# The gates' bias, added by matmuls or by accumulating transfers, in a one-core hybrid mixer layer

## The chip, the core and the metric

The kernel runs on one core of a Trainium2 chip. The metric is the device time of one execution in microseconds (us); lower is better. Five engines work from queues of their own, each in its queue's order: TensorE (PE in the profile, its weight loads PEld), VectorE (DVE), ScalarE (ACT), GpSimd (POOL) and SyncE (SP). They wait for each other, and for transfers, through semaphores.

## The reference, cut to what matters

One decoder layer on 256 tokens of width 2048: four token mixers run on a normalised, modulated input `h`, each is projected to 2048 channels and multiplied by a gate of its own, and the sum goes through an output projection and a SwiGLU feed-forward part. The gates are what the change is about:

```
h = _rms(x, norm_g[l, 0]) * (1.0 + scale_m) + shift_m
merged = [jax.nn.sigmoid(h @ w_gate[l, i] + b_gate[l, i]) * (branches[i].astype(h.dtype) @ w_branch[l, i])
          for i in range(N_BRANCH)]
mix = (merged[0] + merged[1] + merged[2] + merged[3]) @ w_out[l]
```

`w_gate` is four matrices of 2048 x 2048, and `b_gate` four rows of 2048, one number for each channel and the same for every token.

## The kernel before, in words

**Matmuls in three parts.** Every weight comes from HBM as f32 in pieces of 128 x 2048 (1 MB), issued by SP in `load` (L121) into a ring of three tiles `raw`. `split` (L126) cuts a piece into two chunks of 1024 columns: ScalarE casts the chunk to a rounded tile `whi` (L137), VectorE takes the remainder `wlo` (L138, written by the helper `tt` at L75). Four pairs of such tiles are kept, with a fifth while the mixers run. `mm3t` (L265) then makes three matmuls of 128 x 128 by 512 columns for each 128 rows of weights and each half of the tokens: high by high, high by low, low by high. All matmuls are issued by the helper `mm` at L96.

**Stages.** First the input projection in four rounds (L317 to L365), in which the chunks of `h`, called `hx`, are made as well. Then the stage that matters here, from 284 to 840 us of the span. `gates(i)` (L899) runs 16 gate units for branch `i`. A unit (`gate_unit`, L825) is one quarter `kq` of the contraction for one of four groups `ng` of 512 output channels: 24 matmuls of 512 columns into two banks of PSUM, one for each half of the tokens. Between the units the mixers are driven in small steps: `serial` (attention, mLSTM and GLA, one after the other), `s5` (the state space mixer), and dot products for the modulation rows (`ada_tile`, L191, 2.28 us of VectorE each). `branch_unit` (L852) projects a finished mixer and multiplies it by its gates. The order is `gates(0)`, `gates(1)`, branch units of 0 and 1, `gates(2)`, branch units of 2, `gates(3)`, branch units of 3. From 840 us on come the output projection and the feed-forward part, which the change doesn't touch.

**The gates' bias before.** `gate_bias` (L305), called once in the second round of the input projection, clears a tile `braw`, loads the 16 rows of 512 biases as two halves of 256 columns, and makes `bhl`, 32 rows of high parts and 32 of remainders for each half, with a tile `bsel` of zeros and ones that picks a row. At the start of each group (`kq == 0`) `gate_unit` opens each bank with two matmuls of 256 columns that write the bias of that group for all 128 tokens (L831 to L835). The weights' matmuls add to that.

**After a group's last unit** (`kq == 3`) ScalarE copies both banks into a tile `sig` (L843, 128 x 512 each), and a sigmoid of 128 x 1024 in place follows on ScalarE (L846, by the helper `act` at L93). There are 16 such tiles, four for each branch. `branch_unit` reads them on VectorE much later.

**What sets the order.** The code is not the order of the queues. A scheduler places each instruction by a priority, which follows the code, and by when it thinks that its operands are ready; so the sigmoid, which the code writes after all four groups of a branch, stands right behind its own group's copies in the queue. The numbers behind names (sig_4263) are instances, counted by the program as it is built. Semaphores in the queues are named by what they wait for: PE, DVE, Activation (ScalarE), DMAHW (SP's transfers), DMASW (GpSimd's transfers).

Of the kernel before, what the change touches and what calls it, by code (L numbers as in the profile page):

```python
# [11 lines left out]
F32R = mybir.dt.float32r  # L12
# [7 lines left out]
P = 128  # L20
# [49 lines left out]
def trunk(ctx: ExitStack, tc: tile.TileContext, A: dict, out: bass.AP):  # L70
    nc = tc.nc
    ve, se, te, sy = nc.vector, nc.scalar, nc.tensor, nc.sync

    def tt(o, a, b, op):
        return ve.tensor_tensor(out=o, in0=a, in1=b, op=op)  # L75
# [19 lines left out]
    def mm(o, l, r, start, stop):  # L95
        return te.matmul(o, lhsT=l, rhs=r, start=start, stop=stop, skip_group_check=True)  # L96

    MUL, ADD, SUB, MAX, MIN = ALU.mult, ALU.add, ALU.subtract, ALU.max, ALU.min
# [8 lines left out]
    def mmtile():  # L107
        return pmm.tile([P, 512], F32, name="mmt", tag="mmt")
# [39 lines left out]
    def weights(src, pool=None, nb=NB, tag=None):  # L148
        return split(load(src), pool, nb, tag)
# [17 lines left out]
    mxc = mixers.enter_context(tc.tile_pool(name="mxc", bufs=1))  # L167
# [4 lines left out]
    def f4t(name):  # L172
        return f4.tile([P, 4, 256], F32, name=name, tag="f4")
# [5 lines left out]
    for q in range(4):  # L179
        t = f4t(f"xt{q}").rearrange("p a b -> p (a b)")  # L180
# [19 lines left out]
    def take_ada(n):  # L200
        for _ in range(n):
            if todo:
                ada_tile(*todo.pop(0))
# [24 lines left out]
    for j in range(0, NK, 2):  # L228
        ps = mmtile() if j % 4 == 0 else mxtile()
        for n in range(2):  # L230
            for tok in range(2):
                src = xt[2 * tok + (j + n) // 8]
                c = (j + n) % 8 * P
# [4 lines left out]
    hx = []  # L238
# [26 lines left out]
    def mm3t(o, whl, xhl, tok, start, stop):  # L265

        wh, wl = whl
        xh = xhl[:, tok * P : tok * P + P]
        xl = xhl[:, 256 + tok * P : 256 + tok * P + P]
        mm(o, xh, wh, start, False)  # L270
        mm(o, xh, wl, False, False)
        mm(o, xl, wh, False, stop)
# [24 lines left out]
    def need(j):  # L297
        while len(hx) <= j:
            next(chunk_steps)


    bhl = mxc.tile([P, 256], F32R, name="bhl")
    bsel = mxc.tile([P, 32], F32R, name="bsel")

    def gate_bias():  # L305
        t = f4t("braw").rearrange("p a b -> p (a b)")
        ve.memset(t, 0.0)
        for q in range(4):
            sy.dma_start(t[32 * q : 32 * q + 16, 0:256], A["b_gate"][q // 2])
        sy.dma_start(t[:, 512:544], A["bsel"])  # L310
        se.copy(bsel, t[:, 512:544])
        se.copy(t[:, 256:512].bitcast(F32R), t[:, 0:256])
        for q in (0, 64):
            se.copy(bhl[q : q + 32, :], t[q : q + 32, 0:256])
            tt(bhl[q + 32 : q + 64, :], t[q + 32 : q + 64, 0:256], t[q + 32 : q + 64, 256:512], SUB)

    k0 = 0  # L317
    for r, kr in enumerate(ROUNDS):
        last = r == len(ROUNDS) - 1
        ahead = 0 if last else 3 * ROUNDS[r + 1]  # L320
        rest = GROUPS
        if r == 0:
            lead, rest = GROUPS[:NLEAD], GROUPS[NLEAD:]
            lb = dict(held)
            lb["da_q"] = [mmtile(), mmtile()]
            lb["da_k"] = [mmtile(), ps5.tile([P, 512], F32, name="hs2", tag="ys")]
            for k in range(kr):
                need(k)
                raw = load(A["w_lead"][k])
                x = xq[k // 4][:, k % 4, :]  # L330
                for g, gname in enumerate(lead):
                    for b in range(2):
                        mm(lb[gname][b], x[:, b * P : b * P + P], raw[:, g * 512 : g * 512 + 512], k == 0, k == kr - 1)
            for gname in lead:
                if gname not in held:
                    group_out(gname, lb[gname], True)
        need(k0 + kr - 1)
        for i, gname in enumerate(rest):
            g = GROUPS.index(gname)
            gets = [weights(A[f"w_in{r}"][g - NLEAD if r == 0 else g][:, c : min(c + 2048, kr * 512)]) for c in range(0, kr * 512, 2048)]  # L340

            def get(off, width):
                return gets[off // 2048](off % 2048, width)

            keep = gname in held
            banks = held[gname] if keep else [mmtile(), mmtile()]
            group_mm(banks, get, [(k, k0 + k) for k in range(kr)], r == 0 or not keep, True)
            if not keep or last:
                group_out(gname, banks, r == 0 or keep)
            if last:  # L350
                take_ada(AW[i])
            for _ in range(ahead * (i + 1) // len(rest) - ahead * i // len(rest)):
                next(chunk_steps)
        get = weights(A[f"w_sm{r}"])
        bank = mmtile()
        for k in range(kr):
            mm2(bank, get(k * P, P), hx[k0 + k], k == 0, k == kr - 1)
        if r == 0:
            se.copy(small, bank[:, 0:256])
        else:  # L360
            tt(small, bank[:, 0:256], small, ADD)
        tt(small, bank[:, 256:512], small, ADD)
        if r == 1:
            gate_bias()
        k0 += kr  # L365


# [454 lines left out]
    def by_token(t):  # L822
        return t.rearrange("p a b -> p (a b)").rearrange("p (t f) -> p t f", t=2)

    def gate_unit(i, n):  # L825

        ng, kq = divmod(n, 4)
        get = weights(A["w_gate"][i, ng, kq])
        if kq == 0:
            gate_unit.banks = [mmtile(), mmtile()]  # L830
            for bank in gate_unit.banks:  # L831
                c = 4 * i + ng
                for q in range(2):
                    mm(bank[:, q * 256 : q * 256 + 256], bsel[:, q * 16 + c : q * 16 + c + 1].broadcast_to([P, P]),
                       bhl, q == 0, False)  # L835
        for tok, bank in enumerate(gate_unit.banks):
            for k in range(4):
                mm3t(bank, get(k * 512, 512), hx[4 * kq + k], tok, False, kq == 3 and k == 3)
        if kq == 3:
            t = f4t(f"sig{i}{ng}")  # L840
            sig[i, ng] = t
            for tok, bank in enumerate(gate_unit.banks):
                se.copy(by_token(t)[:, tok, :], bank)  # L843
        if n == NK - 1:
            for q in range(4):
                act(sig[i, q], sig[i, q], AF.Sigmoid)  # L846
# [252 lines left out]
    for q in range(4):  # L1099
        t = hxp.tile([P, 512], F32, name="gf", tag="hx")  # L1100
# [31 lines left out]
def layout(i):  # L1132

    f = np.float32
    c_ = np.ascontiguousarray
    a = {}
# [36 lines left out]
    for r, kr in enumerate(ROUNDS):  # L1173
# [3 lines left out]
        if r == 0:  # L1177
# [3 lines left out]
        k0 += kr  # L1181
    a["w_gate"] = c_(np.asarray(i["w_gate"], f)[0].reshape(4, 4, 4, P, 4, 512).transpose(0, 4, 1, 3, 2, 5)
                     .reshape(4, 4, 4, P, D))
    a["b_gate"] = c_(np.asarray(i["b_gate"], f).reshape(16, 2, 256).transpose(1, 0, 2))
    bs = np.zeros((P, 32), f)
    bs[:16, :16] = bs[32:48, :16] = bs[64:80, 16:] = bs[96:112, 16:] = np.eye(16, dtype=f)
    a["bsel"] = bs
    a["w_branch"] = c_(np.asarray(i["w_branch"], f)[0].reshape(4, 4, P, 4, 512).transpose(0, 3, 2, 1, 4)
                       .reshape(4, 4, P, D))
    a["w_out"] = c_(np.asarray(i["w_out"], f)[0].reshape(4, 4, P, 4, 512).transpose(3, 0, 2, 1, 4)  # L1190
# [64 lines left out]
```

## Time and profile before

| | |
|---|---|
| time, median of 3 runs | 1672.57 us (1669.89 to 1672.8) |
| the profiled execution | 1672.82 us, of which its span 1671.0 us |
| PE busy, share of the span | 1625.8 us, 97% |
| VectorE busy | 1190.6 us, 71% |
| ScalarE busy | 840.7 us, 50% |
| GpSimd busy | 0.2 us, 4 instructions |
| bytes moved, mean rate | 401.62 MB, 240 GB/s |

The span runs from the first to the last instruction. A busy PE is not a PE at its peak, since matmuls are pipelined and their ends are modelled: a matmul of 512 columns is shown as 0.39 us, while in a row they follow each other every 0.23 us. So the tables by stage, and where the chain of waits (the work that ended last, followed back) runs through PE, say more than the share over the span.

### The profile page before, as it was taken

How to read it: one execution, taken by the hardware profiler on the slowest of the kernel's cores; microseconds unless marked ns; L12 is line 12 of the kernel's file. 1: busy time of each engine (PE TensorE's matmuls, PEld its weight loads, DVE VectorE, ACT ScalarE, POOL GpSimd, SP SyncE). 2: the span in 40 equal slices, each digit the busy share in tenths (PEclk: the TensorE clock that was granted, in tenths of full speed). 3: DMA queues.
4: the chain of work that ended last, by engine and by line, in shares of the span. 5: the costliest groups of instructions: out<-in, count | busy, mean ns of one | idle time of the engine just before them, and what ended most of it. 6: DMA issues, size and time to landing. Idle time of an engine off the chain costs nothing.

```text
span 1671.0 us, 19012 instructions
## 1 busy us (share of the span) xinstructions
PE 1625.8 (97%) x7344; PEld 1307.9 (78%) x7344; DVE 1190.6 (71%) x1578; ACT 840.7 (50%) x1135; POOL 0.2 (0%) x4
## 2 busy tenths in 40 slices
PE   5999999999999999999999899999999999999997
PEld 3678888777777777777888688888888888888886
DVE  6689989899899998987656755656565545444444
ACT  3544455678765366365446644444444444444432
POOL 0000000000000000000000000000000000000000
PEclk9999999999999999999999999999999999999999
DMA  9988887775567775775476456666666555655553
GB/s 388 377 317 322 332 336 275 281 261 205 212 210 265 284 264 198 259 264 207 177 254 250 151 201 235 244 238 240 242 229 227 184 200 180 223 184 195 201 185 119
DMA packets 61122, 401.62 MB, mean 240 GB/s; under 512 B 6879, under 2 KB 10468, under 8 KB 13416
## 3 DMA queue, kind: packets, MB, share of 16 engines
q1 hardware_dynamic: 60456, 399.37, 65.4%
q8 instruction: 57, 0.93, 0.2%
q10 hardware_dynamic: 576, 1.05, 0.2%
q14 instruction: 33, 0.27, 0.0%
HBM read 398.27 MB, written 2.12 MB: 240 GB/s over the span
## 4 chain that ended last, share of the span: by engine, by line
PE 83%; DVE 11%; ACT 3%; issue 2%; DMA 1%; SPq 0%; DVEq 0%; ACTq 0%
PE mmt L96 76%; PE mxt L96 4%; DVE wlo L75 3%; PE hs L96 2%; DVE raw L83 1%; ACT whi L137 1%; DVE pc L75 1%; DVE pc L790 1%; DMA raw<-in_w_gate 1%; DVE pq L75 1%; DVE xc L75 1%; ACT L93 1%; PE mxt L1070 1%; PE ys L96 1%; DVE sig L75 1%
## 5 line engine op out<-in xcount | busy, mean ns | idle before, releaser
L75 DVE TENSOR_TENSOR wlo<-raw,whi 128x1024 fp32r<-128x1024 f32 x540 | 652.6, 1217 | 391.9 <-ACT whi L137 376.5
L137 ACT CAST whi<-raw 128x1024 fp32r<-128x1024 f32 x540 | 560.5, 1048 | 578.5 <-PE mmt L96 481.9
L96 PE MATMUL mmt<-whi,hx 128*128 128x512 f32 x1568 | 501.0, 395 | 2.7 <-ACT whi L137 2.6
L96 PE MATMUL mmt<-whi,h 128*128 128x512 f32 x1408 | 439.2, 392 | 1.6 <-DVE h L75 0.8
L96 PEld LDWEIGHTS mmt<-whi,hx 128*128 128x128 f32 x1568 | 294.9, 189 | 70.0 <-issue 6.4
L96 PE MATMUL mmt<-wlo,hx 128*128 128x512 f32 x784 | 308.7, 394 | 4.5 <-DVE wlo L75 4.5
L96 PEld LDWEIGHTS mmt<-whi,h 128*128 128x128 f32 x1408 | 264.5, 188 | 58.6 <-DVE h L75 2.4
L96 PE MATMUL mmt<-wlo,h 128*128 128x512 f32 x704 | 274.4, 390 | 0.0
L83 DVE SCALAR_TENSOR_TENSOR raw<-raw,cb 128x2048 f32<-128x2048 f32 x96 | 218.8, 2283 | 1.9 <-DMA raw<-in_ada 1.6
L96 PE MATMUL mmt<-whi,hid 128*128 128x512 f32 x704 | 217.3, 389 | 0.0
L96 PEld LDWEIGHTS mmt<-wlo,hx 128*128 128x128 f32 x784 | 148.1, 189 | 38.4 <-DVE wlo L75 7.9
L96 PEld LDWEIGHTS mmt<-wlo,h 128*128 128x128 f32 x704 | 132.7, 188 | 27.0
L96 PEld LDWEIGHTS mmt<-whi,hid 128*128 128x128 f32 x704 | 132.1, 188 | 27.4
L96 PE MATMUL mmt<-wlo,hid 128*128 128x512 f32 x352 | 136.9, 389 | 0.0
L96 PE MATMUL mmt<-whi,os 128*128 128x512 f32 x256 | 82.9, 399 | 0.2 <-ACT whi L137 0.2
L96 PE MATMUL mmt<-whi,mx 128*128 128x512 f32 x256 | 79.3, 390 | 0.0
L93 ACT ACT_TABLE_LOAD x58 | 74.4, 1283 | 6.2 <-DVE fx L80 2.9
L96 PEld LDWEIGHTS mmt<-wlo,hid 128*128 128x128 f32 x352 | 66.1, 188 | 13.8
L96 PEld LDWEIGHTS mmt<-whi,os 128*128 128x128 f32 x256 | 48.0, 188 | 13.3 <-ACT whi L137 1.0
L96 PEld LDWEIGHTS mmt<-whi,mx 128*128 128x128 f32 x256 | 48.1, 188 | 9.8
L96 PE MATMUL mmt<-wlo,os 128*128 128x512 f32 x128 | 51.3, 401 | 1.8 <-DVE wlo L75 1.8
L96 PE MATMUL mmt<-wlo,mx 128*128 128x512 f32 x128 | 50.1, 391 | 0.0
(290 smaller groups left out, 1044.0 us busy)
## 6 DMA issues: line engine op xcount, KB each, us to landing
raw<-in_ada SPq DMA_DIRECT2D x96, 1024.0 KB, 5.1
raw<-in_ffn_in SPq DMA_DIRECT2D x88, 1024.0 KB, 5.0
raw<-in_w_gate SPq DMA_DIRECT2D x64, 1024.0 KB, 5.0
raw<-in_ffn_out SPq DMA_DIRECT2D x44, 1024.0 KB, 4.9
raw<-in_w_in SPq DMA_DIRECT2D x40, 1024.0 KB, 6.6
raw<-in_w_branch SPq DMA_DIRECT2D x16, 1024.0 KB, 4.9
raw<-in_w_out SPq DMA_DIRECT2D x16, 1024.0 KB, 4.9
raw<-in_w_lead SPq DMA_DIRECT2D x4, 1024.0 KB, 14.2
```

The lines of the kernel that those rows point to most:

```text
L75: return ve.tensor_tensor(out=o, in0=a, in1=b, op=op)
L83: return ve.scalar_tensor_tensor(out=o, in0=a, scalar=s, in1=b, op0=op0, op1=op1, accum_out=accum)
L93: return se.activation(out=o, in_=i, func=f, **kw)
L96: return te.matmul(o, lhsT=l, rhs=r, start=start, stop=stop, skip_group_check=True)
L137: se.copy(hi[:, :n], s)
L790: ve.tensor_tensor_scan(out=pc[:, c, :], data0=mg, data1=pc[:, c, :], initial=0.0, op0=MUL, op1=ADD)
L1070: te.transpose(ps[:, n * 256 + tok * P : n * 256 + tok * P + P], sa[tok][:, c : c + P], ident)
```

## The change

`gate_bias`, `bhl`, `bsel` and the 64 bias matmuls are taken out, and the first weight matmul of a group opens the bank. Once ScalarE has copied a bank into its half of `sig`, GpSimd issues a transfer that reads a row of 512 biases from HBM for each of the 128 partitions and adds it to that half in SBUF (`accum_op=ADD`): 32 transfers of 256 KB, two for each tile `sig`.

```diff
-    bhl = mxc.tile([P, 256], F32R, name="bhl")
-    bsel = mxc.tile([P, 32], F32R, name="bsel")
-
-    def gate_bias():
-        t = f4t("braw").rearrange("p a b -> p (a b)")
-        ve.memset(t, 0.0)
-        for q in range(4):
-            sy.dma_start(t[32 * q : 32 * q + 16, 0:256], A["b_gate"][q // 2])
-        sy.dma_start(t[:, 512:544], A["bsel"])
-        se.copy(bsel, t[:, 512:544])
-        se.copy(t[:, 256:512].bitcast(F32R), t[:, 0:256])
-        for q in (0, 64):
-            se.copy(bhl[q : q + 32, :], t[q : q + 32, 0:256])
-            tt(bhl[q + 32 : q + 64, :], t[q + 32 : q + 64, 0:256], t[q + 32 : q + 64, 256:512], SUB)
...
-        if r == 1:
-            gate_bias()
...
             gate_unit.banks = [mmtile(), mmtile()]
-            for bank in gate_unit.banks:
-                c = 4 * i + ng
-                for q in range(2):
-                    mm(bank[:, q * 256 : q * 256 + 256], bsel[:, q * 16 + c : q * 16 + c + 1].broadcast_to([P, P]),
-                       bhl, q == 0, False)
         for tok, bank in enumerate(gate_unit.banks):
             for k in range(4):
-                mm3t(bank, get(k * 512, 512), hx[4 * kq + k], tok, False, kq == 3 and k == 3)
+                mm3t(bank, get(k * 512, 512), hx[4 * kq + k], tok, kq == 0 and k == 0, kq == 3 and k == 3)
...
             for tok, bank in enumerate(gate_unit.banks):
                 se.copy(by_token(t)[:, tok, :], bank)
+                nc.gpsimd.dma_start(by_token(t)[:, tok, :], A["b_gate"][i, ng : ng + 1, :].broadcast_to([P, 512]),
+                                    accum_op=ADD)
```

How the queues change is told at three places. The first is TensorE's queue at the start of the gate stage, before: the end of the projection's small matmuls (`hx,whi`, `hx,wlo`), the four bias matmuls of the first group, then its weights.

```order
825 L96 MATMUL mmt<-hx,wlo 128x256
826 L96 MATMUL mmt<-hx,whi 128x512
827 L96 MATMUL mmt<-hx,wlo 128x256
828 L96 MATMUL mmt<-bhl,bsel 128x256 [waits DVE_49]
829 L96 MATMUL mmt<-bhl,bsel 128x256
830 L96 MATMUL mmt<-bhl,bsel 128x256 [waits DVE_49]
831 L96 MATMUL mmt<-bhl,bsel 128x256
832 L96 MATMUL mmt<-whi,hx 128x512 [waits Activation_49]
833 L96 MATMUL mmt<-wlo,hx 128x512
```

The same place in the changed kernel:

```order
827 L96 MATMUL mmt<-hx,wlo 128x256
828 L96 MATMUL mmt<-hx,whi 128x512
829 L96 MATMUL mmt<-hx,wlo 128x256
830 L96 MATMUL mmt<-whi,hx 128x512 [waits DVE_49,Activation_49]
831 L96 MATMUL mmt<-wlo,hx 128x512 [waits DVE_49]
832 L96 MATMUL mmt<-whi,hx 128x512 x2
```

The weights' matmuls stand where the bias matmuls stood, and the first of them now takes over the wait for the banks.

The second place is ScalarE's queue around the last group of branch 1, before. The copies, the load of the sigmoid's table and the sigmoid follow each other; behind them come the casts of the next weights.

```order
426 L843 COPY sig_4263<-mmt 128x512 [waits PE_49]
427 L137 CAST whi<-raw 128x1024 [waits PE_49]
428 L843 COPY sig_4263<-mmt 128x512 [waits PE_49]
429 L93 ACT_TABLE_LOAD
430 L93 ACTIVATE sig_4263<-sig_4263 128x1024 [waits Activation_49]
431 L137 CAST whi<-raw 128x1024 [waits DMAHW5_49]
432 L137 CAST whi<-raw 128x1024 [waits DVE_49,PE_49]
```

The same group in the changed kernel, where it is sig_4230:

```order
426 L820 COPY sig_4230<-mmt 128x512 [waits PE_49]
427 L137 CAST whi<-raw 128x1024 [waits DMAHW6_49]
428 L137 CAST whi<-raw 128x1024 [waits PE_49]
429 L820 COPY sig_4230<-mmt 128x512 [waits PE_49]
430 L93 ACT_TABLE_LOAD [waits DMASW7_49]
431 L93 ACTIVATE sig_4230<-sig_4230 128x1024 [waits DMASW6_49]
432 L137 CAST whi<-raw 128x1024 [waits DMAHW0_49]
433 L137 CAST whi<-raw 128x1024 [waits DVE_49,PE_49]
```

The table load waits for the second half's transfer (DMASW7) and the sigmoid for the first half's (DMASW6); the casts behind them stand where they stood.

The third place is GpSimd's queue, in which before nothing stood between the start and the end of the program. Around the same group it now holds, with sig_3972 the group ahead:

```order
18 L821 DMA sig_3972<-in_b_gate 128x512 [waits DMASW4_49,DVE_49,Activation_49]
19 L821 DMA sig_3972<-in_b_gate 128x512 [waits DMASW5_49,Activation_49]
20 L821 DMA sig_4230<-in_b_gate 128x512 [waits DMASW6_49,Activation_49]
21 L821 DMA sig_4230<-in_b_gate 128x512 [waits DMASW7_49,Activation_49]
22 L821 DMA sig_4782<-in_b_gate 128x512 [waits DMASW0_49,DVE_49,Activation_49]
```

Each transfer waits for ScalarE's copy of its half, and nothing else stands in that queue. At the other groups the scheduler puts between none and 18 of ScalarE's other instructions between the second copy and the table load, and the places of other instructions on all queues move by a few rows from the second round of the projection on. The loads of activation tables on ScalarE number 58 before and 60 in the changed kernel.

## Rows read from the trace of the kernel before

**Rows 1.** Stages of the mixer part: start:end, us; busy us and instructions of PE, PEld, DVE, ACT
```profile
284.00:532.00 248.00, 246.31 (x1271) 192.71 (x1269) 225.90 (x418) 184.12 (x319) 0.00 (x0) 1.00 0.67 237
...
701.00:774.00 73.00, 69.00 (x309) 54.18 (x308) 67.70 (x104) 41.48 (x50) 0.00 (x0) 0.98 0.68 245
774.00:840.00 66.00, 65.99 (x306) 53.60 (x305) 42.70 (x63) 33.31 (x51) 0.00 (x0) 1.00 0.54 196
```

**Rows 2.** Chain of waits: shares in 284 to 532 and 774 to 840; pieces in 701 to 774
```profile
by line: PE mmt L96 57.6%; PE mxt L96 12.8%; DVE wlo L75 3.2%; ACT L93 2.6%; ACT whi L137 2.3%; issue 2.1%; DVE pc L790 1.9%; PE ys L96 1.5%; PE mxt L399 1.5%; DVE pc L75 1.3%; PE bu L96 1.1%; DVE gatt L646 1.0%; PE mxt L410 1.0%; DVE pq L7
...
by line: PE mmt L96 84.4%; PE mxt L96 10.5%; PE mxt L876 5.5%; issue 0.0%
...
704.90 5.85 DMA raw<-in_w_gate
...
714.33 7.26 DMA raw<-in_w_gate
```

**Rows 3.** Timeline of PE at the first group: start, us, engine, line, op
```profile
284.37 0.28 PE L96 MATMUL mmt<-hx,wlo 128*128 128x256 f32 x1
284.48 0.62 PE L96 MATMUL mmt<-bhl,bsel 128*128 128x256 f32 x4
284.94 0.40 PE L96 MATMUL mmt<-whi,hx 128*128 128x512 f32 x1
```

**Rows 4.** The bias matmuls alone by stage: start:end, us; PE busy (instructions), PEld
```profile
284.00:532.00 248.00, 5.92 (x32) 4.62 (x32) 0.00 (x0) 0.00 (x0) 1.00 0.67 237
...
622.00:677.00 55.00, 1.36 (x8) 1.14 (x8) 0.00 (x0) 0.00 (x0) 1.00 0.57 204
...
701.00:774.00 73.00, 2.01 (x10) 1.38 (x9) 0.00 (x0) 0.00 (x0) 0.98 0.68 245
```

**Rows 5.** Instructions of the tile braw: ns min/median/max, first and last start
```profile
L314 ACT CAST bhl<-braw x2: 398/400/402, 149.2 to 149.7; 32x256 fp32r<-32x256 f32 x2
L307 DVE MEMSET braw<- x1: 912/912/912, 95.4 to 95.4; 128x1024 f32 x1
L312 ACT CAST braw<-braw x1: 408/408/408, 150.1 to 150.1; 128x256 fp32r<-128x256 f32 x1
```

**Rows 6.** Chain of waits in 150 to 162: start, us, what
```profile
158.28 0.40 DVE bhl L75
...
158.70 0.42 DVE bhl L75
```

**Rows 7.** DMA issues: queue, count, KB each, median us from issue to landing
```profile
raw<-in_w_sm SPq DMA_DIRECT2D x4, 256.0 KB, 5.0
...
gf<-rowd SPq DMA_DIRECT2D x4, 256.0 KB, 7.1
out_x<-x SPq DMA_DIRECT2D x4, 256.0 KB, 2.5
...
cd<-in_s_c SPq DMA_DIRECT2D x4, 128.0 KB, 3.6
```

**Rows 8.** Timeline of ACT at three groups' sigmoids: start, us, what, [idle before]
```profile
400.99 1.28 ACT L93 ACT_TABLE_LOAD   x1
402.29 1.06 ACT L93 ACTIVATE sig<-sig 128x1024 f32<-128x1024 f32 x1
403.25 1.03 ACT L137 CAST whi<-raw 128x1024 fp32r<-128x1024 f32 x1
...
528.50 1.06 ACT L93 ACTIVATE sig<-sig 128x1024 f32<-128x1024 f32 x1
530.80 1.04 ACT L137 CAST whi<-raw 128x1024 fp32r<-128x1024 f32 x1 [1.25 <-DMA raw<-in_w_branch]
...
682.21 1.06 ACT L137 CAST whi<-raw 128x1024 fp32r<-128x1024 f32 x1 [3.43 <-DMA raw<-in_w_branch]
```

**Rows 9.** Groups of DVE in 284 to 840: busy us, mean ns
```profile
L80 DVE TENSOR_SCALAR fx<-iota,sp 128x256 f32<-128x256 f32 x16 | 5.5, 344 | 5.4 <-ACT cs L93 5.4
```

**Rows 10.** Page, DMA queue of the loads: packets, MB, share of 16 engines
```profile
q1 hardware_dynamic: 60456, 399.37, 65.4%
```

More of the change, by code (lines that the diff above doesn't have):

```diff
@@ L1183, in layout @@
                      .reshape(4, 4, 4, P, D))
[L1184 to L1187, printed above, removed]
+    a["b_gate"] = c_(np.asarray(i["b_gate"], f).reshape(4, 4, 512))
     a["w_branch"] = c_(np.asarray(i["w_branch"], f)[0].reshape(4, 4, P, 4, 512).transpose(0, 3, 2, 1, 4)
```

## The prediction

> **What bounds the kernel now.** I read the page first: PE is busy for 97% of the span. Since a busy PE may still wait, I then read the chain of waits and the stages of the mixer part, 284 to 840 us, where all that the change touches lies, but for a small preparation. In 284 to 532, which holds the gate groups of branches 0 and 1, the chain runs mostly through PE's own matmuls, and VectorE is busy for 225.9 of 248 us, so it is close behind [rows 1, 2]. In 701 to 774 the chain runs through the state space mixer's steps on VectorE and ScalarE and through two waits for loaded gate weights, 5.85 and 7.26 us; PE has gaps there [rows 1, 2]. In 774 to 840 PE is the bound again, with 65.99 of 66 us [rows 1, 2]. ScalarE is busy for 184.1 of 248 us in the first stretch [rows 1], but it stands between all others: each weight chunk and most mixer steps pass through its queue, which runs in order.
>
> **What goes: the bias matmuls.** The four matmuls of the first group begin at 284.48, and the weights' matmul behind them at 284.94, so a group costs 0.46 us [rows 3], and 16 groups 7.4 us. (The busy time of such rows is more, as each row also holds the fill of the pipeline.) This counts where PE sets the end. Eight groups, 32 matmuls, lie in 284 to 532; two lie in 622 to 677 and two more in 701 to 774, where the chain is VectorE's [rows 4]; the other four lie at stretches of PE. I take 12 groups, 5.5 us, with 0 and 7.4 as ends: 0 if VectorE, close behind, takes over.
>
> **What goes: the preparation.** The memset of 0.91 us, three casts of together 1.2 us [rows 5], a small fourth, and two subtractions on VectorE of together 0.82 us; these last stand on the chain at 158 us [rows 6]. Five issues leave SP's queue, which the chain does not touch there. I take 1.2 us: the 0.82 and some of the memset. Ends: 0, and 2.9 for all of these.
>
> **What is new: a wait on ScalarE.** The transfers themselves run on GpSimd's empty queue and on the DMA engines, beside everything else. Their price is that the sigmoid, and in the queue already the load of its table, waits until the second half's transfer has landed. Behind the waiting table load stand casts of the next weights, for which VectorE's `wlo` and then PE wait, and the mixers' small copies and exponentials, for which PE's next products and VectorE wait. Two things set the price.
>
> First, the cover: ScalarE's work between the second copy and the table load, counted over the order of the changed kernel with the durations of the trace (cast 1.03, table load 1.28 [rows 8]; 0.41 for 256 columns [rows 5]). Of the 16 groups three have 3.8 us or more. The other 13 have 0 to 2.2 us, on the mean 1.3; at the group shown ahead, sig_4230, it is 0. The table load, which hid nothing before, hides nothing now, as it waits itself.
>
> Second, the landing, from the copy's end to the semaphore. The trace of before has no accumulating transfer and none from GpSimd. The nearest rows by size: 256 KB written at the program's end, with little else under way, landed in 2.5 us; 256 KB of weights in mid-stream in 5.0, as part of one queue; four broadcasts of 256 KB at once in 7.1; and 128 KB for the state space mixer, issued in this very stage, in 3.6 [rows 7]. I take 4.3 us, between the row of this stage and the one of this size in mid-stream, and keep 2.5 and 7.1 as ends.
>
> ScalarE then waits 13 x (4.3 - 1.3) + 0.5 = 39.5 us in all, 3.0 us at a time. How much of that reaches the end? Behind the sigmoids, ScalarE of before had nothing to wait for in one of the three shown places, 1.25 us in the second and 3.43 us in the third [rows 8]: on the mean 1.6 of the 3.0 are idle time that is only moved. Of the rest some is caught by chunks that lie ready: 12 matmuls of 0.23 us, 2.7 us for each. Mixer steps have no such stock. I take a quarter of the whole, 9.9 us; the ends are nothing and all of it.
>
> **Smaller terms.** Two more table loads of 1.28 us [rows 8], by the same quarter 0.6 us. The new traffic: 32 x 256 KB are 8.4 MB; the load queue's 399.37 MB took 65.4% of 1671 us [rows 10], so 8.4 MB take 23 us of all 16 engines, and twice that if the read of the destination counts like the source. That is 4 to 8% of the 556 us of the stage; of the 13.1 us that the chain waits for gate weights in 701 to 774 [rows 2] it adds some 0.7 us. VectorE's products with the gates come long after the sigmoids and wait for nothing new. That the scheduler moves other rows by a few places I price at nothing, with 2 us either way.
>
> **The sum.** -5.5 - 1.2 + 9.9 + 0.6 + 0.7 = +4.5 us on the profiled execution's 1672.82, which is 0.25 above the median of the runs: 1677 us against 1672.57.
>
> **The rivals.**
>
> *Not slower: the landing is as short as in an empty queue.* At 2.5 us the waits sum to 13 x 1.2 = 15.6 us, on the mean shorter than the idle time that two of the three shown places have; a sixth, 2.6 us, might pass. With the whole 7.4 us of PE and 1.7 us of VectorE's preparation back, and 0.8 for the smaller terms, the sum is -5.7: 1667 us. For it speaks the write of 2.5 us [rows 7]; against it, that this write met no other traffic, while the DMA engines are busy for 0.67 of 284 to 532 [rows 1]. It decides at a landing of about 3.5 us, where a quarter of the waits, 7 us, is as much as the 6.7 us that the removals give. The Trainium skill, page "DMA: Bandwidth & Descriptors", section "Anatomy of one DMA — SWDGE (gpsimd) path", fits transfers from GpSimd as 2.0 us plus the bytes at 436 GB/s, which makes an estimate of 2.6 us here and would lead to this rival's 1667; no row of before shows such a transfer.
>
> *Even: the landing is 3.0 to 3.9 us,* as the 3.6 of the transfers in this stage [rows 7]. A quarter of 22 to 34 us is 6 to 9 us, against 6.7 and the smaller terms: 1671 to 1676.
>
> *Much slower: the landing is 5.5 us or more.* The waits of 56 us then outlast the idle time at each shown place, and I let 30% pass: 17 us, net +12, 1684; at 7.1 us it is 79 us of waits and 1693 or more. For it speaks that an addition must read its destination too; against it, that these transfers have a queue of their own and are not behind the 1 MB loads. VectorE taking over as the bound (the 5.5 us not given back) ends in the same region, at 1682.5.
>
> VectorE's other work is weighed for the landing as well: its kind of scalar operation with the longest time in this stage, `fx`, takes 344 ns and 5.5 us in all [rows 9]. The Trainium skill, page "SBUF — State Buffer", section "SBUF: two separate sides", warns that transfers from GpSimd are held up while VectorE runs an operation in a two-port mode; were every transfer held by such a row, the sum would be 13 x 0.34 / 4 = 1.1 us more, 1678, and by the rows alone it stays at 1677.
>
> **How the numbers follow.** Forecast (landing 4 to 5.5 us) 0.30, even 0.28, not slower 0.27, much slower 0.15. The difference that a measurement of this kernel can tell is about 0.2%, 3.3 us. So faster has 0.27, same 0.28, slower 0.45, and the likeliest is 1677 us, with a range of its own of 1675.9 to 1683. The range of 1667 to 1688 leaves out about half of the case below (0.13) and the longest landings (0.07).
>
> **What would show it.** In the profile after: 32 issues on GpSimd's queue with a median landing, which decides; ScalarE's waits at the load of the sigmoid's table or at the sigmoid, released by a transfer into `sig`, about 40 us in all if the landing is 4.3; PE's busy time in 284 to 532 shorter by some 4 us if waits don't fill it; no wait of 158 us' kind on `bhl`. The prediction is wrong if the landing is under 3.5 us, if ScalarE waits long and PE still shows no new gaps (then the quarter is too much), or if the input projection or the feed-forward part change by more than 2 us.

## The result, and the profile after

The changed kernel takes 1734.97 us at the median of 4 runs (1725.26 to 1739.01), the kernel before 1671.94 (1669.89 to 1672.8): a ratio of 1.037, with an interval of 1.0326 to 1.0414. It is 63 us slower, where +4.5 was forecast. The profiled execution took 1739.01 us, its span 1737.2.

The page of the changed kernel: the busy time of PE, the bytes on GpSimd's queue, the loads of ScalarE's tables (busy us, mean ns, then idle time before them and its releaser), and the landing of the new transfers (KB each, median us):

```profile
PE 1643.1 (95%) x7280; PEld 1312.7 (76%) x7280; DVE 1192.1 (69%) x1575; ACT 838.4 (48%) x1133; POOL 28.2 (2%) x36
...
q0 software_dynamic: 4608, 8.39, 3.0%
...
L93 ACT ACT_TABLE_LOAD x60 | 77.0, 1283 | 91.8 <-DMA sig<-in_b_gate 80.7
...
sig<-in_b_gate POOLq DMA_DIRECT2D x32, 256.0 KB, 6.7
```

The new transfers land in 6.7 us, at the median of all 32. A table load with 80.7 us of idle time ahead of it is new. The table of waits of the changed kernel (engine, line, what it waited for: us in total, times, the longest) holds all of it:

```profile
DVE wlo L75 <- ACT whi L137: 437.0, 204, 12.0
...
ACT L93 <- DMA sig<-in_b_gate: 80.7, 13, 10.4
...
ACT sig L93 <- DMA sig<-in_b_gate: 5.4, 1, 5.4
```

ScalarE waits 86.1 us in 14 places, and VectorE, which needs ScalarE's casts, 437.0 us in place of 376.5. The stages of the changed kernel, with the columns of [rows 1] (PE's busy time comes first, its granted clock and the share of the DMA engines near the end):

```profile
0.00:282.00 282.00, 260.66 (x1086) 202.08 (x1087) 238.00 (x296) 130.31 (x165) 0.20 (x4) 0.99 0.88 338
282.00:906.00 624.00, 564.26 (x2546) 434.61 (x2545) 497.02 (x809) 343.76 (x524) 28.02 (x32) 0.95 0.68 226
906.00:1737.00 831.00, 818.21 (x3652) 675.97 (x3651) 457.09 (x472) 364.33 (x446) 0.00 (x0) 0.99 0.58 209
```

The same stage of the kernel before:

```profile
282.00:840.00 558.00, 548.33 (x2618) 430.57 (x2616) 496.09 (x812) 346.41 (x524) 0.00 (x0) 1.00 0.67 239
```

So all of the loss lies in the mixer stage, 624 us in place of 558. What follows it lasts 831 us in the one and 1671 - 840 = 831 us in the other. VectorE and ScalarE have as much work as before (497.0 and 343.8 us against 496.1 and 346.4), PE has its 64 bias matmuls less, and yet it is idle for 60 us in place of 10 and its granted clock is 0.95 in place of 1.00.

**One place shows the mechanism.** It is the fifth group, sig_3391. ScalarE of the changed kernel (start, us, what, in brackets its idle time before and the releaser):

```profile
438.95 0.58 ACT L820 COPY sig<-mmt 128x512 f32<-128x512 f32 x1 [0.31 <-PE mmt L96]
...
441.39 0.37 ACT L393 COPY o<-mxt 128x256 f32<-128x256 f32 x1 [0.55 <-PE mxt L392]
449.46 1.28 ACT L93 ACT_TABLE_LOAD   x1 [7.70 <-DMA sig<-in_b_gate]
...
451.72 1.97 ACT L137 CAST whi<-raw 128x1024 fp32r<-128x1024 f32 x2
453.60 0.64 ACT L393 COPY o<-mxt 128x256 f32<-128x256 f32 x2
```

GpSimd there, and the landings of its two transfers:

```profile
437.09 0.86 POOL L821 DMA_DIRECT2D sig<-in_b_gate  x1 [31.04 <-ACT sig L820]
439.83 1.02 POOL L821 DMA_DIRECT2D sig<-in_b_gate  x1 [1.89 <-ACT sig L820]
...
DMA to landing us min/median/max: 4.4/7.0/9.6
```

The second copy ends at 439.53, GpSimd issues its transfer at 439.83, and the table load begins at 449.46, 9.6 us later. ScalarE stands still for 7.70 us of these. The first half's transfer took 4.4 us, the second's 9.6, and the second is the one that the table load waits for. It is so in 14 of the 16 groups: the first halves land in 5.5 us on the mean, the second in 8.0 (5.4 to 10.0). Why the second is slower no run shows. Behind the table load wait two casts and a copy of an attention result. VectorE and PE there:

```profile
452.78 2.36 DVE L75 TENSOR_TENSOR wlo<-raw,whi 128x1024 fp32r<-128x1024 f32 x2 [6.93 <-ACT whi L137]
```

```profile
446.89 0.63 PE L96 MATMUL mmt<-whi,hx 128*128 128x512 f32 x2
454.01 2.08 PE L96 MATMUL mxt<-small,wa 128*128 128x256 f32 x4 [6.49 <-ACT o L393]
...
457.59 1.05 PE L96 MATMUL mmt<-whi,hx 128*128 128x512 f32 x2
458.44 0.63 PE L96 MATMUL mmt<-wlo,hx 128*128 128x512 f32 x1
...
460.33 0.62 PE L96 MATMUL mmt<-whi,hx 128*128 128x512 f32 x2
460.79 0.39 PE L96 MATMUL mmt<-wlo,hx 128*128 128x512 f32 x1
```

PE's ready chunks last until 447.5, 5.8 us beyond ScalarE's halt; then it stands for 6.49 us. And when it comes back, two matmuls take 0.85 us (457.59 to 458.44), where three microseconds later two take 0.46 us (460.33 to 460.79). The granted clock says why, in stretches of 3 us of the changed kernel:

```profile
449.00:452.00 3.00, 0.00 (x0) 0.00 (x0) 0.00 (x0) 2.53 (x3) 0.00 (x0) 1.00 0.69 292
452.00:455.00 3.00, 0.99 (x2) 0.84 (x3) 2.22 (x2) 2.98 (x5) 0.00 (x0) 0.53 0.01 3
455.00:458.00 3.00, 3.00 (x8) 2.34 (x7) 0.14 (x1) 2.82 (x7) 0.00 (x0) 0.50 0.58 183
458.00:461.00 3.00, 3.00 (x12) 2.41 (x11) 2.79 (x3) 2.97 (x4) 0.00 (x0) 0.83 0.42 172
```

After the gap PE is granted 0.50, which is 1.2 of 2.4 GHz, until about 459. So a wait costs twice here: the gap, and the half clock behind it.

**The sum.** Over stretches of 2 us of the mixer stage I added PE's idle time, and its busy time multiplied by one less the granted clock (what the low clock lost). The kernels of the experiments below stand in the same table. Each row is of one profiled execution, which can lie up to 4 us off its kernel's median (those of after and of nobias lie 4.0 and 3.7 us above).

| mixer stage, us | ends at | PE idle | lost at a low clock |
|---|---|---|---|
| before | 840.3 | 9.7 | 1.6 |
| after | 906.1 | 59.7 | 25.9 |
| nobias | 838.0 | 11.4 | 8.0 |
| tiny | 835.0 | 12.1 | 4.7 |
| behind | 840.2 | 17.6 | 3.4 |
| half | 867.5 | 31.8 | 17.4 |
| waittiny | 871.2 | 36.6 | 16.5 |
| waitplain | 876.1 | 36.1 | 20.6 |
| late | 853.2 | 22.1 | 9.3 |
| late2 | 846.3 | 17.9 | 7.9 |
| latetiny | 836.3 | 13.8 | 3.2 |
| dveadd | 867.0 | 31.5 | 15.0 |

From before to after, +50.0 and +24.3 less the 7.4 us of bias matmuls make 66.9, against 66.2 us between the spans. Not all of the last column lies behind long gaps: in nobias PE was granted 0.50 in 490 to 492, after 2 us in which it was idle for 0.28 and ran mostly matmuls of 64 columns.

### The profile page after: what moved, and what is told of

The parts are those of the page before. It is cut to its first block, busy times and chain, and to the rows that moved or that the text cites. A ratio compares the mean times of both kernels' runs of the same rounds, so it can differ in the third digit from the quotient of the medians.

```text
span 1737.2 us, 18995 instructions
## 1 busy us (share of the span) xinstructions
PE 1643.1 (95%) x7280; PEld 1312.7 (76%) x7280; DVE 1192.1 (69%) x1575; ACT 838.4 (48%) x1133; POOL 28.2 (2%) x36
## 3 DMA queue, kind: packets, MB, share of 16 engines
q0 software_dynamic: 4608, 8.39, 3.0%
## 4 chain that ended last, share of the span: by engine, by line
PE 50%; issue 24%; DVE 3%; DMA 1%; ACT 1%; POOL 1%; DVEq 0%; POOLq 0%; ACTq 0%
PE mmt L96 49%; DMA sig<-in_b_gate 1%; POOL sig L821 1%; DVE wlo L75 1%; PE mxt L96 1%; PE mxt L1049 1%; DVE raw L83 0%; DVE x L83 0%; ACT whi L137 0%; ACT L93 0%; DVE mlqc L83 0%; DVE mlkc L83 0%; PE mxt L855 0%; DVE mixt L79 0%; DVE pc L75 0%
## 5 line engine op out<-in xcount | busy, mean ns | idle before, releaser
L75 DVE TENSOR_TENSOR wlo<-raw,whi 128x1024 fp32r<-128x1024 f32 x540 | 653.6, 1219 | 452.3 <-ACT whi L137 437.0
L96 PE MATMUL mmt<-whi,hx 128*128 128x512 f32 x1568 | 509.2, 402 | 4.4 <-ACT whi L137 4.4
L96 PEld LDWEIGHTS mmt<-whi,hx 128*128 128x128 f32 x1568 | 300.5, 193 | 78.3 <-issue 8.8
L96 PE MATMUL mmt<-wlo,hx 128*128 128x512 f32 x784 | 315.0, 402 | 12.3 <-DVE wlo L75 12.2
L93 ACT ACT_TABLE_LOAD x60 | 77.0, 1283 | 91.8 <-DMA sig<-in_b_gate 80.7
L96 PE MATMUL mmt<-whi,os 128*128 128x512 f32 x256 | 87.3, 417 | 3.6 <-ACT whi L137 2.2
```

What stands on the lines that cost most here:

```text
L93: return se.activation(out=o, in_=i, func=f, **kw)
```

## The experiments

Differences below are against the kernel before in the same runs (its medians there lie at 1669.4 to 1671.9): the ratio less one, times 1671 us.

**The removals alone: nobias.** From the changed kernel:

```diff
-                nc.gpsimd.dma_start(by_token(t)[:, tok, :], A["b_gate"][i, ng : ng + 1, :].broadcast_to([P, 512]),
-                                    accum_op=ADD)
```

> The changed kernel without the 32 transfers: the gates' bias is left out of the computation. It is the removal half of the change alone. Theory W (ScalarE waits for the landing, PE then has gaps, and its clock is granted at half behind each gap): everything lost comes with the transfers, so this kernel is 5 to 8 us below the kernel before, 1664 to 1667, its ScalarE has no wait of a sigmoid, PE's idle time in the mixer stage is about 10 us and the time lost at a low clock about 2 us. Rival R (the other order of rows that came with the removal costs the time): 1700 or more also here. Rival T (traffic of the transfers): the same as W here.

Measured: 1667.77 us, ratio 0.9982 (0.9973 to 0.9991), so -3.0 us. The loss comes with the transfers, but the removals gave less than half of what was expected.

**The transfers without the wait: behind.**

```diff
             for q in range(4):
                 act(sig[i, q], sig[i, q], AF.Sigmoid)
+                for tok in range(2):
+                    nc.gpsimd.dma_start(by_token(sig[i, q])[:, tok, :],
+                                        A["b_gate"][i, q : q + 1, :].broadcast_to([P, 512]), accum_op=ADD)
```

(the transfers behind the copies are gone).

> The same 32 transfers with addition, issued behind the sigmoid in place of ahead of it, so that no ScalarE instruction waits for them (the bias is then added after the sigmoid, which is another function than the reference's). Theory W: within 4 us of the run without transfers, 1664 to 1671, although the landing stays at 6 to 7 us. Rival T (the transfers take DMA engines or SBUF from the weights and from the engines): most of the 63 us stays, 1710 or more. Rival R: 1700 or more.

Measured: 1674.27 us, ratio 1.0019 (1.0009 to 1.0029), +3.2 us. The landing on its page, and its mixer stage:

```profile
sig<-in_b_gate POOLq DMA_DIRECT2D x32, 256.0 KB, 7.6
```

```profile
282.00:840.00 558.00, 540.47 (x2546) 421.26 (x2545) 494.57 (x810) 343.68 (x524) 28.34 (x32) 0.99 0.76 253
```

The same 32 transfers, with a landing that is even longer, cost 3.2 us when ScalarE doesn't wait for them, and 62 when it does. So 58.7 of the 62 us come with issuing them ahead of the sigmoid, where ScalarE waits for them. That all of this is the wait is not shown by this run alone, as the place of the transfers changed too; waitplain below keeps the place. The 6.2 us from nobias to here were more than the 4 expected.

**What these 6.2 us are: tiny.** As behind, with `0:1` of the 512 columns in destination and source.

> As the kernel with the transfers behind the sigmoids, in exactly its order of instructions, but each transfer with addition has 1 of the 512 columns, 512 bytes in place of 256 KB (nearly all of the bias is left out). It parts the 6.5 us that lie between the kernel without transfers (1667.8) and the one with them unwaited (1674.3): if the bytes cost them, 1667 to 1669; if the other order of the instructions (or the 32 issues) costs them, 1673 to 1675.

Measured: 1671.22 us, ratio 1.0004 (0.9995 to 1.0013), +0.7 us, between the two. The expectation puts the first part down to another order of instructions; but in the traces nobias, tiny and behind run the same instructions in the same order on every engine except GpSimd. So 3.7 us come with the 32 transfers, however small, and 2.5 with their bytes; each of the two is known to some 2 us. What in a transfer of half a kilobyte costs the 3.7 us no run shows.

**Half of the waits: half.**

```diff
             for tok, bank in enumerate(gate_unit.banks):
                 se.copy(by_token(t)[:, tok, :], bank)
+                if i < 2:
...
                 act(sig[i, q], sig[i, q], AF.Sigmoid)
+                for tok in range(2 if i > 1 else 0):
+                    nc.gpsimd.dma_start(by_token(sig[i, q])[:, tok, :],
+                                        A["b_gate"][i, q : q + 1, :].broadcast_to([P, 512]), accum_op=ADD)
```

> The changed kernel in branches 0 and 1; in branches 2 and 3 the transfers are issued behind the sigmoid, where nothing on ScalarE waits for them (there the bias comes after the sigmoid, which is another function than the reference's). Theory W: the loss goes by the waits that stay. Nine of the 14 waits of the changed kernel lie in branches 0 and 1, so about 50 to 60 percent of the 61 us between the two earlier kernels is left: 1702 to 1713. If the loss came from a few late waits of the last branches instead, this kernel would be under 1690; if from the first waits alone, above 1725.

Measured: 1698.66 us, ratio 1.0169 (1.0153 to 1.0186), +28.2 us; the waits that are left:

```profile
ACT L93 <- DMA sig<-in_b_gate: 31.9, 5, 8.7
```

My count was wrong: six of the 14 waits of the changed kernel lie in branches 0 and 1, with 33.1 of 86.1 us, not nine. Against behind the five waits of 31.9 us cost 25.0 us, and the 86.1 us of the changed kernel cost 58.7: the loss goes by the waits that stay.

**Shorter landings with the wait kept: waittiny and waitplain.** From the changed kernel, one column of the 512; or all 512, without `accum_op=ADD`.

> The changed kernel with its waits, but each transfer has 1 of the 512 columns (nearly all of the bias is left out), which landed in 5.0 us at the median where nothing waited, in place of 6.7 to 7.6. The waits should shrink by some 2 us each, from 86 to about 58 us in 14 places. Fixed part of 3.1 us absorbed per wait: PE's idle time grows by 15 us in place of 42 against the unwaited kernel (1671.2 with these transfers), the low clock adds about 8: 1692 to 1698. Constant share of 0.7 us per us: 1671 + 41 = 1712, that is 1708 to 1716.

> The changed kernel with its waits and its 256 KB transfers, but without the addition (the bias overwrites the gates, which is another function). Unwaited, these landed in 5.4 us at the median. Waits of some 55 to 65 us in all. Fixed part: 1694 to 1704 (unwaited 1673.7 plus 20 to 30). Constant share: 1711 to 1719. If the landing plays no part and the wait as such is what costs: about 1735 as the changed kernel.

Measured: waittiny 1703.23 us, ratio 1.0197 (1.0182 to 1.0213), +32.9; waitplain 1707.77, ratio 1.0215 (1.0196 to 1.0235), +35.9. The waits of waittiny, and of waitplain:

```profile
ACT L93 <- DMA sig<-in_b_gate: 48.5, 12, 8.1
...
ACT sig L93 <- DMA sig<-in_b_gate: 5.4, 1, 5.4
```

```profile
ACT L93 <- DMA sig<-in_b_gate: 55.0, 13, 8.1
...
ACT sig L93 <- DMA sig<-in_b_gate: 2.9, 1, 2.9
```

Waittiny fell between my two expectations; waitplain missed the fixed part's by 4 us, and nearly reached the constant share's. Against the unwaited kernel with the same transfers (tiny +0.7; plain, below, +3.0) the four kernels give

| | waits | us each | loss, us each | difference |
|---|---|---|---|---|
| waittiny | 13 | 4.15 | 2.5 | 1.7 |
| waitplain | 14 | 4.14 | 2.35 | 1.8 |
| after | 14 | 6.15 | 4.2 | 2.0 |
| half | 5 | 6.4 | 5.0 | 1.4 |

On the mean of these kernels a wait of ScalarE costs its own length less 1.4 to 2.0 us. I read it as a fixed part that is absorbed, smaller than the 3.1 us that I had put, while the rest reaches the end, half clock included. A constant share fits less well: it is 0.60 and 0.57 in the first two and 0.68 to 0.78 in the others. The waits are those of the profiled executions and the losses those of medians; with the times of the profiled executions the difference is 0.9 to 1.7 us.

The cleanest pair is waitplain and the changed kernel: they run the same instructions in the same order on every engine, and only the addition is gone. 28.2 us less of waits go with 25.9 us less of time. (In waittiny rows have moved, and ScalarE has two more table loads.)

**What makes the landing: idle, plain, hwq and small.** Idle (1713.44 us, with the landings of its transfers in it) leaves the transfers of the gates out and appends twelve to the end (`xs` is the last output's tile):

```diff
+    row = A["b_gate"][0, 0:1, :].broadcast_to([P, 512])
+    full = A["glu_w"][:, 0:512]
+    for src, accum in ((row, True), (row, False), (full, True), (full, False)):
+        for _ in range(2):
+            ...
+    for src in (row, row, full, full):
+        sy.dma_start(xs, src)
```

Plain is behind without `accum_op=ADD`, hwq is plain with `se.dma_start`, small is behind with 128 columns.

> The bias is left out of the gates (no transfer in the mixer stage); behind the last output twelve transfers of 256 KB into one tile follow one another, each waiting for the one ahead, with nothing else on the DMA engines: on GpSimd's queue two broadcasts of a row with addition, two without, two full sources with addition, two without; then on SP's queue two broadcasts and two full sources. Each landing is read from the trace. If the 6.7 us are made by the company of the weight loads, all land in 2.5 to 3.5 us here; if the addition makes them, the two kinds with addition land at least 2 us after those without; if GpSimd's queue makes them, SP's land at least 2 us sooner than GpSimd's. The sum of the landings, 30 to 80 us, is added to the end of the run.

> As the kernel with the transfers behind the sigmoids, from GpSimd's queue, but without the addition (the gates are overwritten, which is another function). Only the landing is asked, against 7.6 us with the addition: if the addition's read of the destination makes it, 4 to 5.5 us here; if the queue or the company of the weight loads makes it, within 1 us of 7.6.

> Transfers without addition, from ScalarE's queue, behind the sigmoids, same tile, source and size as in the changed kernel (they overwrite the gates, which is another function). Nothing waits for them but the products. Only the landing is asked: if GpSimd's queue or the addition makes the 6.7 to 7.6 us, they land in 3 to 5 us here; if the weight loads on the shared DMA engines make it, in 6 us or more.

> As the kernel with the transfers behind the sigmoids, with addition, but 128 of the 512 columns, 64 KB in place of 256 KB (part of the bias is left out and the rest comes after the sigmoid). Only the landing is asked, against 7.6 us: if it goes by the bytes, 2.5 to 4 us; if it is mostly a fixed price or waiting behind weight loads, 6 us or more.

Measured: the issues of idle at its end, median us to landing:

```profile
x<-in_glu_w POOLq DMA_DIRECT2D x4, 256.0 KB, 3.7
x<-in_b_gate SPq DMA_DIRECT2D x2, 256.0 KB, 3.2
```

The chain of idle's last stretch tells the kinds apart:

```profile
1666.13 4.09 DMA x<-in_b_gate
...
1670.52 3.95 DMA x<-in_b_gate
...
1674.76 3.54 DMA x<-in_b_gate
...
1678.59 3.48 DMA x<-in_b_gate
...
1682.36 4.11 DMA x<-in_glu_w
```

Alone, 256 KB land in 4.0 to 4.1 us with the addition, whether the source is one row or 128, and without it in 3.5 from one row and 3.2 to 3.3 from 128. In the mixer stage:

| transfer, unwaited | queue | landing, median us | time of one run (before beside it) |
|---|---|---|---|
| 256 KB, addition (behind) | GpSimd | 7.6 | see above |
| 256 KB, no addition (plain) | GpSimd | 5.4 | 1673.65 (1670.64) |
| 256 KB, no addition (hwq) | ScalarE | 5.3 | 1672.03 (1669.42) |
| 64 KB, addition (small) | GpSimd | 5.6 | 1672.27 (1670.64) |
| 0.5 KB, addition (tiny) | GpSimd | 5.0 | see above |

No single cause makes it: plain came out as expected for the addition, hwq and small between the two answers that were expected of them. GpSimd's queue is not it: ScalarE's is as slow (hwq's trace tells 20 of the 32 landings). Being in the stage is a part: 3.5 becomes 5.4, and even half a kilobyte takes 5.0. The addition costs 0.5 us alone and 2.2 in the stage, or 1.4 where ScalarE waits (6.7 against waitplain's 5.3). Such a transfer makes 4608 packets with the addition and 2560 without, for the same 8.39 MB. What in the stage a transfer of 0.5 KB waits for, no run shows.

**The sigmoid moved away from its transfers: late, late2 and latetiny.** The gates are complete in the first two.

```diff
+    def late_sigmoid(behind):
+        for t in due:
+            with tc.issue_after(behind.ins):
+                act(t, t, AF.Sigmoid)
+        due.clear()
...
-                se.copy(by_token(t)[:, tok, :], bank)
+                c = se.copy(by_token(t)[:, tok, :], bank)
...
+            late_sigmoid(c)
+            due.append(t)
```

Late2 calls it at `kq == 3` of the next group, behind that unit's last cast. Latetiny is late with one column.

> The changed kernel complete, but each sigmoid stands behind the next group's second copy on ScalarE (for the last group of branches 1 to 3 behind the cast of the fourth branch weights), some 30 us after its transfers, so that they have landed. Theory W: no wait of ScalarE for a transfer above 1 us, PE's idle time in the mixer stage back to 10 to 15 us, 1664 to 1672, which is level with or a little better than before. Rival T: 1710 or more. Rival R: 1700 or more.

> The changed kernel complete, with each sigmoid behind the last cast of the next group's fourth weights on ScalarE, some 10 us behind its transfers instead of 30. Theory W with a second part, that ScalarE's order matters by itself: no long wait for a transfer, and a time between the 1674 of the kernel with the transfers behind the sigmoids and the 1686 of the later sigmoids: 1670 to 1680. Rival, that any displacement of the sigmoid costs some 12 us: 1683 to 1690.

> The kernel with the latest sigmoids (behind the next group's second copy, 1686.0 us) in exactly its order of instructions, each transfer with 1 of the 512 columns (nearly all of the bias is left out). Nothing waits for the transfers in either. If the order of the instructions makes the 12 us over the kernel with the transfers behind the sigmoids, 1680 to 1686; if the bytes make them, 1671 to 1675.

Measured: late 1686.02 us, ratio 1.0089 (1.0075 to 1.0103), +14.9; late2 1676.23, 1.0032 (1.002 to 1.0044), +5.3; latetiny 1669.02, 0.9988 (0.9975 to 1.0002), -2.0. In none of them ScalarE waits for a transfer into `sig`. My expectation for late failed, and what I then thought, that the order of ScalarE makes the 15 us, failed too: in the same order without the bytes they are gone. The waits for loads in the mixer stage, of late:

```profile
ACT whi L138 <- DMA raw<-in_w_gate: 57.6, 24, 5.6
...
ACT whi L138 <- DMA raw<-in_w_branch: 37.7, 11, 9.2
...
DVE raw L83 <- DMA raw<-in_ada: 10.4, 4, 2.9
```

and of latetiny:

```profile
ACT whi L138 <- DMA raw<-in_w_gate: 51.0, 21, 8.1
...
ACT whi L138 <- DMA raw<-in_w_branch: 34.5, 10, 6.9
...
DVE raw L83 <- DMA raw<-in_ada: 1.3, 2, 0.7
```

and of late2, for ScalarE:

```profile
ACT whi L138 <- DMA raw<-in_w_gate: 64.8, 28, 5.3
...
ACT whi L138 <- DMA raw<-in_w_branch: 33.6, 9, 7.4
```

Late and latetiny run the same instructions in the same order, so the 16.9 us between them are the bytes'. Their waits for loads differ by about as much, 105.7 against 86.8 us, but that is not the price: late2 has ScalarE wait for loads just as long, 98.4 us against late's 95.3, and is 9.6 us faster. So that the bytes cost by the loads that they delay is likely, and not shown. The same bytes cost 2.5 us in behind, where each is issued after its sigmoid; why the place matters so much is open. What part of the changed kernel's own loss is of this kind is open too. Without the addition it is small: waitplain, with all the bytes, waits 57.9 us in all and waittiny 53.9, and 3.0 us lie between their times.

**VectorE in place of ScalarE: dveadd.** The bias goes plainly into `sig` at `kq == 0`, and

```diff
-                se.copy(by_token(t)[:, tok, :], bank)
-                nc.gpsimd.dma_start(by_token(t)[:, tok, :], A["b_gate"][i, ng : ng + 1, :].broadcast_to([P, 512]),
-                                    accum_op=ADD)
+                tt(t[:, tok, :], bank, t[:, tok, :], ADD)
```

> No addition in the transfers: one plain transfer of 512 KB from GpSimd's queue puts the bias into the gates' tile at the start of a group, and VectorE adds the PSUM bank to it in place of ScalarE's copy. ScalarE loses 32 copies of 0.58 us, VectorE gains 32 additions of some 0.6 to 0.7 us, about 21 us. Theory W: no wait of ScalarE for a transfer, but VectorE, busy 225.9 of 248 us in the gates of branches 0 and 1, is nearly full: between 1665 (hidden) and 1688 (all of it on the path); I expect 1675. Rival T: 1710 or more.

Measured: 1696.72 us, ratio 1.0158 (1.0142 to 1.0173), +26.4. VectorE's sums and products with the bank, 64 rows of which 32 are new (busy us, mean ns | idle before), and PE's costliest wait in 282 to 870, with ScalarE's waits for weights:

```profile
L75 DVE TENSOR_TENSOR sig<-mmt,sig 128x512 f32<-128x512 f32 x64 | 43.5, 683 | 10.5 <-PE mmt L96 10.3
```

```profile
PE mmt L96 <- DVE wlo L75: 14.6, 12, 2.7
...
ACT whi L137 <- DMA raw<-in_w_gate: 62.0, 28, 6.4
ACT whi L137 <- DMA raw<-in_w_branch: 52.6, 10, 9.7
```

32 x 0.683 = 21.9 us of work on the engine that is close behind PE, and 26.4 us more of time, of which the clock took its part (15.0 us lost). It is slower than I put its worst. That the additions alone make it is not shown: the kernel also has 8.4 MB of transfers at the groups' starts, and ScalarE waits 114.6 us for gate and branch weights, where before it waited 36.8 and 35.2. The loss can be in part of the kind that late has.

**The bias matmuls' worth: thin64,** from the kernel before:

```diff
-                    mm(bank[:, q * 256 : q * 256 + 256], bsel[:, q * 16 + c : q * 16 + c + 1].broadcast_to([P, P]),
-                       bhl, q == 0, False)
+                    mm(bank[:, q * 256 : q * 256 + 64], bsel[:, q * 16 + c : q * 16 + c + 1].broadcast_to([P, P]),
+                       bhl[:, 0:64], q == 0, False)
```

> The kernel before, in its own order on ScalarE, VectorE and SP, with its preparation, but each of the 64 bias matmuls has 64 of the 256 columns (three quarters of the bias are left out; the banks' other columns are not started anew). By the 0.46 us of a group PE has 16 x 0.345 = 5.5 us less work. If what the removal of the matmuls is worth is their time on PE and only the other order gave 3.7 of 6.7 us back, this kernel is 4 to 5.5 us below before; if VectorE, close behind, takes PE's place as the bound and the time cannot be had, within 2 us of before.

Measured: 1671.58 us, ratio 1.0005 (0.9995 to 1.0015). It settles nothing, since the edit took little of the time out. PE of thin64 at the first group:

```profile
282.78 0.53 PE L96 MATMUL mmt<-bhl,bsel 128*128 128x64 f32 x4
283.15 0.48 PE L96 MATMUL mmt<-whi,hx 128*128 128x512 f32 x1
```

Four matmuls of 64 columns last 0.37 us, of 256 columns 0.46 [rows 3]: 1.4 us in all 16 groups, not 5.5.

## Why the prediction was wrong

The direction and the mechanism were the predicted ones: ScalarE stands at the sigmoid's table load until the transfer has landed, and casts and mixer steps queue behind it. The time was outside the range, by 47 us above its upper end. In the order of its own steps:

- **The removals** (-6.7 forecast): -3.0 measured, between the sum's two ends; that VectorE, close behind, kept the rest is not shown. How much of it is matmuls, preparation or moved rows is not settled: thin64 left most of the matmuls' time in; the first group begins 2.0 us earlier in the changed kernel, but 0.5 in nobias, and 1.7 in thin64, which keeps the preparation, so that the 1.2 us for it cannot be read out. In nobias' profiled execution, its slowest, the low clock takes 8.0 us of the mixer stage in place of 1.6.
- **The cover** (1.3 us on the mean, at 13 groups) held roughly: from the copy's end to the wait, 11 groups have 1.6 us on the mean and five 3.8 or more, two of which don't wait at all.
- **The landing was the first wrong step:** 4.3 us taken, 6.7 measured at the median, and 8.0 on the mean of the second halves, which are the ones that ScalarE waits for; that is beyond the upper end of 7.1. The prediction names the second half, but prices both alike, and all rows that it rested on [rows 7] were of transfers without an addition. With 8.0 its formula gives 13 x 6.7 = 87 us of waits, and 86.1 were measured; that it comes so near is partly luck, given the cover. Where nothing waits, the addition makes 2.2 of 7.6 us. The Trainium skill, page "DMA: Bandwidth & Descriptors", section "Anatomy of one DMA — SWDGE (gpsimd) path", fits such a transfer at an estimated 2.6 us; no run here shows so little: for this size on that queue the least is 3.2 alone, and 5.3 at the median in the stage, both without the addition.
- **The quarter was the second, and the dearest.** Against behind, 42 of the 86.1 us became idle time of PE (59.7 less 17.6), a half and not a quarter, and the low clock added 22.5. The step before it agrees with the runs: I had read off that ScalarE had 1.6 us to spare behind the sigmoids [rows 8], from three places, and 1.4 to 2.0 us of each wait are what the runs show as absorbed. The error was to let ready chunks catch most of what was left. They do carry PE for some microseconds, as the place above shows, but ScalarE and VectorE are then behind by the length of the wait; that they have too little spare time to make the stock again is how I read it, and not shown apart. By 1.7 us absorbed, even the landing that I took would have given 13 x 1.3 = 17 us in place of 9.9, and 1684 us in all.
- **The clock was left out of the sum.** Of the 66 us of the span, 24 are PE's work at half clock. The kernel before shows it once: a granted clock of 0.98 in 701 to 774 [rows 1], where PE has a gap. I read that row for the chain alone.
- **The smaller terms** (0.7 for traffic, 0.6 for table loads): 2.5 us for the bytes where nothing waits, and 16.9 in another order. The 3.7 us of transfers without their bytes were not in the sum.
- **The rivals.** "Much slower" had the right condition, a landing of 5.5 us or more, and a third of the price: at 7.1 us it gave 1693 (its own terms add up to 1691), as it let 30% pass and knew no clock. It had 0.15. ("Even", at a landing of 3.0 us, is 1673 by its own terms, and not 1671.) That VectorE's operations in a two-port mode hold the transfers up, the rule of the Trainium skill's page "SBUF — State Buffer", section "SBUF: two separate sides", finds no support in the trace: the longest landing, 10.0 us from 838.76 on, had VectorE at work for 1.32 us of it.

```profile
838.76:848.77 10.01, 10.01 (x46) 8.36 (x45) 1.32 (x4) 0.00 (x0) 0.86 (x1) 1.00 0.68 230
```


Of the signs that the prediction named, the 32 issues, the waits at the table load and the missing wait on `bhl` came; the waits were 86 in place of 40 us, and PE had long new gaps; its busy time in the mixer stage was longer, not shorter. The part ahead of the mixer stage changed by 2.0 us (its first matmul begins at 282.44 in place of 284.48), the part behind it by less than 1 us.

No version here beats the kernel before with the bias complete: late2 comes nearest, 5.3 us above it. Without any bias work nobias is 3.0 us below it, so in this order about that is all that could be had.

## What to carry to other kernels

Where other engines live off an in-order queue, as here off ScalarE's, price a new wait in it by the landing of the very transfer that is waited for (with its addition, in its stage, the second of two), less what other work covers; here each wait then cost its length less 1.4 to 2.0 us, and no small share of it. If PE runs dry, add the time at half clock, here half as much again as the gaps. And added bytes have no fixed price: 8.4 MB cost 2.5 us in one order and 16.9 in another.

## What was not expected of the hardware

- The addition in a transfer costs 0.5 us alone and 2.2 us in the mixer stage (4.0 and 3.5 us; 7.6 and 5.4).
- Of two such transfers of a group, the first lands in 5.5 us on the mean, the second in 8.0.
- In this stage a transfer of 0.5 KB lands in 5.0 us, one of 256 KB without addition in 5.4: the bytes are the smaller part.
- GpSimd's and ScalarE's queue land the same transfer, without addition, in 5.4 and 5.3 us.
- Four matmuls of a quarter of the columns last 0.37 in place of 0.46 us.
